# The pace of a second stream of work in a mixer: 1.2 of its steps for each step, where 0.89 were

## The chip, the cores and the metric

The kernel runs on one core of one Trainium2 chip. The metric is the time of one execution on the device in microseconds (us). Three executions of the kernel before took 3313.83, 3315.23 and 3316.35 us, so the median is 3315.23 us.

## What is computed

A transformer block (attention, a gated unit, a feed-forward net) works on `x`, 256 tokens of width 1024. Then two layers of a second network work on `x` and on a context `ctx` of 256 tokens. Each layer is a mixer and a layer of experts. Only the first of the two updates the context, and the mixer of the second layer needs the updated context for its keys and values. Cut to what matters:

```python
for i in range(2):
    update_ctx = i < 1
    x, ctx = mixer_sublayer(x, ctx, ...)      # attention, Fourier and convolution branches, three gates
    x = x + gt2 * peer_ffn(modulate(rmsnorm_2(x, g), sh2, sc2), ...)
    if update_ctx:
        ctx = ctx + cgt2 * peer_ffn(modulate(rmsnorm_2(ctx, g), csh2, csc2), ...)

def peer_ffn(h, ...):                          # per token 8 heads x 16 of 16384 experts
    eid, gate = top-16 of the product keys     # route
    u = jnp.take(u_tab, eid, axis=0)
    act = gelu(einsum('chkd,cd->chk', u, hc)) * gate
    v = jnp.take(v_tab, eid, axis=0)
    return einsum('chk,chkd->cd', act, v)
```

## The kernel before

All work is written as Python generators whose steps are recorded one after the other. There are two streams. The main stream takes `x` through the block and the two layers. The side stream takes the context through the first layer; it is advanced a step at a time between steps of the main stream (`alongside`, line 252). How many side steps a main step lets in is a number of the table `PACE` by phase: the first where the main step split a block of weights, the second where it did not (the steps of attention). A credit is added up, and a side step runs for each whole unit. The recorded instructions are then put in an order for each engine by a scheduler with a timeline of its own, so that instructions stand where that timeline had them, not strictly where they were recorded; each engine works through its queue in that order.

Phases that the text speaks of, with the stretch of the profiled execution that each fills:

- **First mixer** (`mix0`, 855 to 1166 us): `_mixer`, line 1012. Products with weights in blocks of 512 KB: each is loaded by the SP queue, split into a high part by ACT (line 364) and a low part by DVE (line 373), and multiplied in three passes on PE (lines 379 to 381, helper `mm3`). The branches (gates, Fourier, convolution) are woven with attention, whose eight heads go in two halves of four (`attend`, line 858: scores line 869, softmax lines 643 to 647, transposes line 540, outputs line 880). The outputs are merged and projected (lines 1082 and 535).
- **Routing** (`route0`, 1166 to 1354 us): a norm, a query product, scores (line 1124) and the top-16 search on DVE (lines 1091 to 1177). The scores of the first experts (tile `pre`, weights `uT`) are pulled forward by the scheduler and keep PE busy here.
- **Gates** (`gate0`, 1354 to 1506 us): for each of 32 groups of 8 tokens DVE builds one-hot tiles (lines 1373, 1374) and weighs them (line 1376, twice), PE multiplies them (line 1382), ACT evicts them (line 1384). The result goes to DRAM (`G`) and is read back in tiles `Gq`.
- **Dense experts** (`dense`, 1506 to 2165 us): products with `Gq` (line 1415), 128 blocks of `v` and the remaining score blocks on PE.
- **Second mixer** (`mix1`, 2165 to 2478 us): as the first. Its attention needs the keys of the updated context. So its attention is woven in only once the side stream has passed the word "keys" (`self.ready`, and `weave`, line 266, at half a step of attention for each step of the branches); whatever is left of attention when the branches end follows after them. The word comes after the very last piece of the context's experts.

The side stream in these phases, for two tiles of 128 tokens (`context_peer`): for each of 128 picks a row of `u` per token is fetched by an indirect DMA that POOL issues (line 1221, 512 KB each, tile `ug`, four buffers) and DVE reduces it (line 1234, `gather_acts`); then the rows of `v` are fetched and summed. For tile 0 the sum is made on PE (line 1289, tile `gacc`: a pair of fetches, then four matmuls, with line 1277 and 1304 on DVE around them). For tile 1 it is made on DVE (line 1254, one instruction for a fetch). The keys of tile 0 (`keys_tile`, line 934) come before the sum of tile 1, the keys of tile 1 at the end, and then the word "keys". A step of the side stream holds one fetch. A fetch also waits for the last split of weights that the main stream had recorded (`behind`, line 292), so that the pace holds on the chip too.

A mixer has 76 steps, 54 with a split of weights and 22 without (4 of keys, 4 of queries and 8 of heads, and 6 of the convolution).

Of the kernel before, what the change touches and what calls it, by code (L numbers as in the profile page):

```python
# [24 lines left out]
NCAND = 112  # L25
GSCALE = 2.0 ** 15
GATHER = (0,)
PACE = {"b1": (2.15, 2.48), "ffn": (1.8, 2.2), "mix0": (0.89, 0.89), "route0": (1.47, 1.25), "gate0":
        (1.16, 0.29), "pre0": (0.9, 1.4), "out0": (1.0, 2.8), "mix1": (0.7, 0.85)}
LOW = {"cmix": "V", "croute": "V", "keys": "V", "b1": "V", "b1r": "V", "ffn": "V", "mix0": "V", "route0":  # L30
       "V", "gate0": "V", "pre0": "V", "out0": "V", "mix1": "V", "route1": "P", "gate1": "V", "pre1": "VP",
# [166 lines left out]
class Net:  # L198
# [42 lines left out]
    def alongside(self, lead, side):  # L241

        credit = 0.0
        for step in lead:
            if step is not None:
                side.mark = step.ins
            credit += PACE[self.phase][step is None]
            while credit >= 1.0:
# [1397 lines left out]
```

## Time and profile before

| | |
|---|---|
| median of three executions | 3315.23 us |
| the profiled execution | 3327.51 us |
| its span in the profile | 3325.8 us |
| PE busy | 2955.7 us (89% of the span) |
| DVE busy | 2464.6 us (74%) |
| ACT busy | 1406.6 us (42%) |
| POOL busy | 806.3 us (24%) |
| granted TensorE clock, mean over the span | 0.937 |

The shares are means over stages with different limits. A row of a table by stage has the stretch, its length, and for each engine the time it was busy with the number of instructions in brackets, then the granted share of TensorE's full clock, the mean busy share of the 16 DMA engines and the rate that they moved. A row of waits has the instruction that waited, what it waited for, the total in us, how many times, and the longest. PE is the matmul unit, PEld its loading of weights, DVE the vector engine, ACT the scalar engine, POOL the engine that issues the indirect DMAs, SP the queue that loads weights.

### The profile page before, as it was taken

The numbers are of one execution on the slowest core, as the hardware profiler recorded it, in microseconds if no ns is written. First come the engines' busy times: TensorE is split into PE (matmuls) and PEld (weight loads), VectorE is DVE, ScalarE is ACT, GpSimd is POOL, SyncE is SP. The second block draws the span as 40 slices with busy tenths as digits, with TensorE's granted clock in tenths as the row PEclk, the third lists the DMA queues.
The fourth block names the chain that finished last, engine by engine and source line by source line (L and its number), as shares of the span: only waits on it lengthen the run. The fifth ranks groups of instructions, "written<-read, shape, count | busy, mean of one in ns | idle before, by whom it ended". The sixth has DMA issues, their size and how long they took to land.

```text
span 3325.8 us, 52744 instructions
## 1 busy us (share of the span) xinstructions
PE 2955.7 (89%) x19879; PEld 2532.1 (76%) x19879; DVE 2464.6 (74%) x5129; ACT 1406.6 (42%) x1938; POOL 806.3 (24%) x565
## 2 busy tenths in 40 slices
PE   6889997888799899947999899977889899999998
PEld 4777786778676677835888788866669899888998
DVE  2645659999896468997988788968657897655555
ACT  2444553333434343423445444443534454544443
POOL 0000000344443233433542444511004433000000
PEclk8999988899799889958999999989989999999999
DMA  7776633799987578988998899966444489755664
GB/s 245 252 251 236 214 133 121 274 329 327 361 297 253 187 268 309 341 293 329 378 368 296 324 370 365 356 223 223 140 137 137 146 250 297 264 193 192 211 215 153
DMA packets 289327, 852.87 MB, mean 256 GB/s; under 512 B 25264, under 2 KB 91568, under 8 KB 284592
## 3 DMA queue, kind: packets, MB, share of 16 engines
q1 hardware_dynamic: 147888, 543.16, 46.9%
q0 software_dynamic: 73728, 268.47, 21.9%
q10 hardware_dynamic: 67456, 37.88, 3.8%
q8 instruction: 156, 2.56, 0.3%
q14 instruction: 99, 0.81, 0.1%
HBM read 814.80 MB, written 34.60 MB: 255 GB/s over the span
## 4 chain that ended last, share of the span: by engine, by line
PE 55%; DVE 18%; DMA 14%; issue 8%; ACT 3%; POOL 2%; SPq 0%; ACTq 0%; DVEq 0%; POOLq 0%
PE acc L380 7%; PE acc L381 7%; PE acc L379 6%; PE ps L381 6%; PE ps L379 6%; PE ps L380 6%; DVE wl L373 4%; DMA ug<-in_u_dram,eidi 3%; DMA ug<-in_v_dram,eidT 3%; DMA w<-in_w_in_dram 3%; DVE gz L1234 2%; DMA w<-in_w_mod_dram 2%; PE pre L381 2%; DVE A L1376 2%; PE pre L379 2%
## 5 line engine op out<-in xcount | busy, mean ns | idle before, releaser
L364 ACT ACTIVATE wh<-w 128x1024 fp32r<-128x1024 f32 (+1 forms) x818 | 850.5, 1045 | 1039.4 <-PE ps L380 283.2
L373 DVE TENSOR_TENSOR wl<-w,wh 128x1024 fp32r<-128x1024 f32 (+1 forms) x770 | 928.4, 1207 | 447.8 <-PE ps L381 109.7
L379 PE MATMUL ps<-hh,wh 128*128 128x256 f32 x2304 | 663.9, 289 | 26.1 <-ACT wh L364 11.0
L381 PE MATMUL ps<-hh,wl 128*128 128x256 f32 x2304 | 666.8, 290 | 20.9 <-DVE wl L373 20.5
L380 PE MATMUL ps<-hl,wh 128*128 128x256 f32 x2304 | 659.9, 287 | 3.0 <-DVE hl L524 2.9
L1221 POOL DMA_INDIRECT ug<-in_u_dram,eidi x256 | 347.4, 1357 | 1007.2 <-DVE rstd L480 562.0
L379 PEld LDWEIGHTS ps<-hh,wh 128*128 128x128 f32 x2304 | 447.8, 194 | 54.5 <-issue 18.7
L381 PEld LDWEIGHTS ps<-hh,wl 128*128 128x128 f32 x2304 | 447.1, 194 | 45.0 <-DVE wl L373 31.2
L380 PEld LDWEIGHTS ps<-hl,wh 128*128 128x128 f32 x2304 | 447.7, 194 | 12.6 <-issue 4.9
L380 PE MATMUL acc<-wl,dh 128*128 128x512 f32 x1024 | 409.4, 400 | 23.6 <-DVE wl L373 23.5
L379 PE MATMUL acc<-wh,dh 128*128 128x512 f32 x1024 | 404.7, 395 | 14.3 <-ACT dh L523 12.2
L381 PE MATMUL acc<-wh,dl 128*128 128x512 f32 x1024 | 403.5, 394 | 0.5 <-DVE dl L524 0.5
L1234 DVE SCALAR_TENSOR_TENSOR gz<-ug,htok 128x1024 bf16<-128x1024 f32 x256 | 310.6, 1219 | 19.8 <-DMA ug<-in_u_dram,eidi 19.4
L381 PE MATMUL pre<-hh,wl 128*128 128x256 f32 x1024 | 299.5, 296 | 19.8 <-DVE wl L373 11.6
L379 PE MATMUL pre<-hh,wh 128*128 128x256 f32 x1024 | 292.5, 287 | 0.1
L380 PE MATMUL pre<-hl,wh 128*128 128x256 f32 x1024 | 292.4, 287 | 0.0
L1221 POOL DMA_INDIRECT ug<-in_v_dram,eidi x128 | 183.7, 1435 | 326.7 <-ACT wh L364 196.7
L380 PEld LDWEIGHTS acc<-wl,dh 128*128 128x128 f32 x1024 | 194.7, 190 | 76.6 <-DVE wl L373 40.6
L379 PEld LDWEIGHTS acc<-wh,dh 128*128 128x128 f32 x1024 | 194.8, 190 | 56.9 <-ACT dh L523 12.5
L381 PEld LDWEIGHTS pre<-hh,wl 128*128 128x128 f32 x1024 | 198.0, 195 | 40.9 <-DVE wl L373 17.7
L381 PEld LDWEIGHTS acc<-wh,dl 128*128 128x128 f32 x1024 | 194.7, 190 | 39.7 <-DVE dl L524 1.2
L373 POOL TENSOR_TENSOR wl<-w,wh 128x1024 fp32r<-128x1024 f32 x48 | 129.8, 2705 | 390.6 <-ACT wh L364 193.2
(514 smaller groups left out, 5112.2 us busy)
## 6 DMA issues: line engine op xcount, KB each, us to landing
w<-in_uT_dram SPq DMA_DIRECT2D x256, 512.0 KB, 4.7
w<-in_v_dram SPq DMA_DIRECT2D x256, 512.0 KB, 4.4
w<-in_w_in_dram SPq DMA_DIRECT2D x142, 512.0 KB, 4.7
w<-in_w_mod_dram SPq DMA_DIRECT2D x96, 512.0 KB, 5.0
w<-in_w_ff_dram SPq DMA_DIRECT2D x64, 512.0 KB, 5.8
G<-Gs ACTq DMA_DIRECT2D x32, 1024.0 KB, 7.9
Gq<-G SPq DMA_DIRECT2D x32, 1024.0 KB, 7.2
w<-in_w_ada_dram SPq DMA_DIRECT2D x48, 512.0 KB, 4.5
```

Of the source, the lines that this page charges most:

```text
L364: self.step = nc.scalar.activation(hi[:, :n], w[:, :n], AF.Copy)
L373: eng.tensor_tensor(lo[:, :n], w[:, :n], hi[:, :n].bitcast(F32), op=OP.subtract)
L379: mm(out, a[0], b[0], start=start, stop=False, skip_group_check=True)
L380: mm(out, a[0], b[1], start=False, stop=False, skip_group_check=True)
L381: mm(out, a[1], b[0], start=False, stop=stop, skip_group_check=True)
L1221: f = self.nc.gpsimd.indirect_dma_start(out=t, out_offset=None, in_=tab, in_offset=bass.IndirectOffsetOnAxis(ap=idx, axis=0))
L1234: nc.vector.scalar_tensor_tensor(j, ut, 1.0, ht, op0=OP.mult, op1=OP.mult, accum_out=sc[:, k:k + 1])
L1376: nc.vector.tensor_tensor(A2[:, i], ohA, over(gp[:, i, ts]), op=OP.mult)
```

## The change

One entry of the table of paces: in the first mixer 1.2 side steps are let in for a step of the main stream, of either kind.

```diff
-PACE = {"b1": (2.15, 2.48), "ffn": (1.8, 2.2), "mix0": (0.89, 0.89), "route0": (1.47, 1.25), "gate0":
+PACE = {"b1": (2.15, 2.48), "ffn": (1.8, 2.2), "mix0": (1.2, 1.2), "route0": (1.47, 1.25), "gate0":
         (1.16, 0.29), "pre0": (0.9, 1.4), "out0": (1.0, 2.8), "mix1": (0.7, 0.85)}
```

Nothing else is edited. 76 steps at 0.89 let in 67 side steps and at 1.2 let in 91, so from there on the side stream stands 24 steps further at every point, and 24 fewer are left at the end. Of 27 side steps that the second mixer took, it takes 3.

Three places show how the queues of the engines change. The first is PE's queue at the end of attention in the first mixer: `po` and `vc`, `v` are outputs of attention, `oh` and `ol` its split result in the projection that follows, and `gacc<-ug,gz` four matmuls for a pair of fetched rows. Before:

```order
L880 MATMUL po<-cpq,vc_92 64x256 x2
L880 MATMUL po<-cpq,v_9799 64x256 x2
L540 MATMUL ptx<-cst,prob 128x128 x8
L880 MATMUL po<-cpq,vc_92 64x256 x2
L880 MATMUL po<-cpq,v_9799 64x256 x2
L379 MATMUL ps<-oh,wh 128x256 x2
```

The same place in the changed program:

```order
L1289 MATMUL gacc<-ug,gz 32x512 x4
L880 MATMUL po<-cpq,vc_92 64x256 x2
L880 MATMUL po<-cpq,v_9833 64x256 x2
L540 MATMUL ptx<-cst,prob 128x128 x4
L1289 MATMUL gacc<-ug,gz 32x512 x4
L540 MATMUL ptx<-cst,prob 128x128 x4
L880 MATMUL po<-cpq,vc_92 64x256 x2
L880 MATMUL po<-cpq,v_9833 64x256 x2
L1289 MATMUL gacc<-ug,gz 32x512 x4
L379 MATMUL ps<-oh,wh 128x256 x2
```

Pairs of fetched rows now stand among the last heads. Counted over the whole queue, 27 pairs stood ahead of the last projection of the mixer and 32 do now; 31 stood ahead of the norm that begins routing and 39 do now; 35 stood ahead of the first routing score (line 1124) and 47 do now.

The second place is DVE's queue where routing ends and the first one-hot tile of the gates is built (line 1373): `oh` are the one-hots of routing, `iT` and `gp` its results, `wl` a split of weights for the scores, and `gz,sdot<-ug,htok` the reduction of one fetched row of `u`. Before:

```order
L1167 TENSOR_TENSOR oh<-iota16b,abr 128x256 x8
L373 TENSOR_TENSOR wl<-w,wh 128x1024
L1169 TENSOR_TENSOR oh<-oh,i16f 128x256 x8
L373 TENSOR_TENSOR wl<-w,wh 128x1024
L1171 TENSOR_REDUCE i_11408<-oh 128x128
L373 TENSOR_TENSOR wl<-w,wh 128x1024 x2
L1334 CAST iT<-ps 128x128 x2
L1335 TENSOR_SCALAR gT<-ps 128x128
L1336 CAST gp<-gT 128x128
L1337 TENSOR_TENSOR gp<-gT,gp 128x128
L1360 CAST iotaT<-cst 128x256
L1373 TENSOR_TENSOR ohB<-iotaT,iT 128x1024
```

The same place in the changed program:

```order
L1171 TENSOR_REDUCE i_11526<-oh 128x128
L1234 SCALAR_TENSOR_TENSOR gz,sdot<-ug,htok 128x1024 x2
L1334 CAST iT<-ps 128x128 x2
L1335 TENSOR_SCALAR gT<-ps 128x128
L1234 SCALAR_TENSOR_TENSOR gz,sdot<-ug,htok 128x1024 x2
L1336 CAST gp<-gT 128x128
L1234 SCALAR_TENSOR_TENSOR gz,sdot<-ug,htok 128x1024
L1337 TENSOR_TENSOR gp<-gT,gp 128x128
L1234 SCALAR_TENSOR_TENSOR gz,sdot<-ug,htok 128x1024
L1360 CAST iotaT<-cst 128x256
L1234 SCALAR_TENSOR_TENSOR gz,sdot<-ug,htok 128x1024
L1373 TENSOR_TENSOR ohB<-iotaT,iT 128x1024
```

Counted over the queue, no reduction of a row stood in routing and 40 stood between the first one-hot and the last weighing of the gates; now 35 stand in routing and 29 in the gates, 24 more in the two together. In the dense phase 88 of line 1234 and 105 of line 1254 become 64 and 127; in the second mixer 22 of line 1254 become none.

The third place is PE's queue in the second mixer, where the third head of the first half of attention ends: `htok` holds the context's values, `ps<-oh` is the projection after attention and `ps<-hh` a product of the branches. Before:

```order
L540 MATMUL ptx<-cst,prob 128x128 x4
L869 MATMUL sc<-cT,q_22581 128x256
L869 MATMUL sc<-k_22582,q_22581 128x256
L540 MATMUL ptx<-cst,prob 128x128 x4
L379 MATMUL ps<-oh,wh 128x256 x2
L815 MATMUL sc<-wa,cnT 128x512
L380 MATMUL ps<-ol,wh 128x256
L381 MATMUL ps<-oh,wl 128x256
L380 MATMUL ps<-ol,wh 128x256
L381 MATMUL ps<-oh,wl 128x256
L880 MATMUL po<-cpq,htok 64x256 x2
L880 MATMUL po<-cpq,v_22583 64x256 x2
```

The same head in the changed program:

```order
L381 MATMUL ps<-hh,wl 128x256
L379 MATMUL ps<-hh,wh 128x256
L380 MATMUL ps<-hl,wh 128x256
L381 MATMUL ps<-hh,wl 128x256
L379 MATMUL ps<-hh,wh 128x256
L380 MATMUL ps<-hl,wh 128x256
L880 MATMUL po<-cpq,htok 64x256 x2
L880 MATMUL po<-cpq,v_21870 64x256 x2
L540 MATMUL ptx<-cst,prob 128x128 x4
L815 MATMUL sc<-wa,cnT 128x512
L381 MATMUL ps<-hh,wl 128x256
L379 MATMUL ps<-hh,wh 128x256
```

The outputs of all four heads of the first half now stand among products of the branches, where before the branches had ended ahead of them. The second half of attention stands behind the branches in both.

## Rows read from the trace of the kernel before

**Rows 1.** Busy time by stage: the two mixers, routing, gates and dense experts between them.

```profile
855.00:1166.00 311.00, 268.31 (x1803) 205.61 (x1803) 218.31 (x551) 124.17 (x197) 113.24 (x96) 0.91 0.75 267
1166.00:1354.00 188.00, 174.42 (x1298) 141.10 (x1295) 150.52 (x586) 73.03 (x93) 70.47 (x63) 0.94 0.82 293
1354.00:1506.00 152.00, 101.49 (x899) 87.50 (x898) 144.83 (x232) 56.39 (x87) 53.61 (x43) 0.74 0.92 313
1506.00:2165.00 659.00, 617.46 (x3532) 531.47 (x3529) 565.23 (x685) 280.14 (x340) 293.55 (x196) 0.97 0.93 350
2165.00:2478.00 313.00, 259.88 (x1722) 214.43 (x1722) 218.89 (x575) 127.18 (x213) 27.19 (x21) 0.90 0.51 176
```

The columns behind the stretch and its length are PE, PEld, DVE, ACT, POOL, the granted clock, the DMA share and GB/s.

**Rows 2.** What PE waited for in routing and gates, 1166 to 1506 us.

```profile
PE gt L1382 <- DVE A L1376: 48.7, 38, 6.1
```

**Rows 3.** Chain of waits, end of the gates: start, us, what.

```profile
1503.14 1.67 PE gt L1382 x14
...
1529.67 0.50 PE acc L380
```

**Rows 4.** Waits in the second mixer's first half, 2165 to 2310 us.

```profile
POOL ug L1221 <- ACT wh L364: 98.7, 15, 28.9
ACT wh L364 <- DMA w<-in_w_in_dram: 26.4, 12, 6.5
DVE htok L1254 <- DMA ug<-in_v_dram,eidi: 19.7, 8, 6.1
...
ACT mt L517 <- DVE mt L514: 11.0, 2, 9.5
```

**Rows 5.** Busy time of line 1289 alone in the first mixer: PE, PEld.

```profile
855.00:1166.00 311.00, 37.04 (x248) 5.70 (x248) 0.91 0.75 267
```

**Rows 6.** What POOL waited for in the first mixer, the longest two.

```profile
POOL ug L1221 <- ACT wh L364: 50.4, 14, 22.0
POOL ug L1221 <- PE gacc L1289: 40.4, 11, 6.1
```

**Rows 7.** What PE waited for in the first mixer, the longest.

```profile
PE gacc L1289 <- DMA ug<-in_v_dram,eidT: 13.2, 8, 2.4
```

**Rows 8.** First mixer, busy time: last heads of attention, then the projections.

```profile
1074.00:1125.00 51.00, 40.37 (x210) 22.89 (x209) 23.13 (x82) 14.92 (x32) 10.32 (x11) 0.87 0.45 153
1125.00:1166.00 41.00, 37.20 (x297) 32.31 (x296) 23.67 (x31) 14.62 (x16) 13.51 (x10) 0.96 0.69 249
```

**Rows 9.** Busy time of line 1234 alone in the gates: DVE.

```profile
1354.00:1506.00 152.00, 48.71 (x80) 0.74 0.92 313
```

**Rows 10.** DVE at the end of a half sum of the context, in time order.

```profile
1178.49 1.62 DVE L1304 SCALAR_TENSOR_TENSOR cT<-gacc,mod_b_mod,cT 128x64 f32<-128x64 f32 x8
```

**Rows 11.** Busy time at the end of routing.

```profile
1300.00:1354.00 54.00, 50.76 (x408) 41.73 (x405) 45.59 (x117) 20.15 (x23) 24.44 (x20) 1.00 0.89 316
```

**Rows 12.** Dense experts: a stretch without and one with the context's keys.

```profile
1700.00:1800.00 100.00, 96.31 (x596) 84.70 (x595) 88.06 (x117) 44.54 (x54) 44.26 (x30) 1.00 0.98 366
1800.00:1900.00 100.00, 87.91 (x549) 77.45 (x550) 77.05 (x125) 46.04 (x64) 33.58 (x22) 0.98 0.79 286
```

**Rows 13.** Second mixer, busy time in five stretches.

```profile
2165.00:2192.00 27.00, 17.24 (x76) 14.11 (x77) 17.55 (x45) 10.27 (x19) 2.14 (x2) 0.56 0.39 137
2192.00:2258.00 66.00, 59.37 (x450) 53.11 (x449) 47.36 (x96) 26.12 (x41) 13.97 (x11) 0.95 0.75 267
2258.00:2384.00 126.00, 100.00 (x687) 84.28 (x685) 96.52 (x278) 54.64 (x85) 11.08 (x8) 0.92 0.55 187
2384.00:2443.00 59.00, 48.47 (x230) 31.52 (x229) 34.85 (x130) 23.25 (x55) 0.00 (x0) 0.91 0.13 45
2443.00:2478.00 35.00, 34.80 (x289) 31.42 (x287) 22.60 (x30) 12.90 (x15) 0.00 (x0) 1.00 0.65 211
```

**Rows 14.** Chain of waits, second mixer, end of attention's first half.

```profile
2398.73 1.96 PE po L880 x8
```

## The prediction

> **What bounds the kernel now.** I read the page, then busy time by stage, then the waits of each stage that the change reaches, then the chain of waits at its seams. From the table by stage the reader is to see that no engine is the bound throughout [rows 1]. In the dense phase PE is busy 617 of 659 us. In the gates DVE is busy 144.8 of 152 us and PE only 101.5, at a granted clock of 0.74 (1 would be 2.4 GHz throughout, 0.5 is 1.2). In routing and gates PE waited 48.7 us for the weighing on DVE [rows 2]. The dense phase cannot start before the gates have gone to DRAM and back: the last gate product is at 1503.1 us and the first product of the dense phase on the chain at 1529.7 [rows 3]. So a microsecond more of DVE ahead of that seam is a microsecond more of the whole. The mixers are bound by no one engine: the second has PE busy 259.9 of 313 us and DVE 218.9. It carries 23 fetches of the side stream whose reductions stand in DVE's queue and wait there for their rows, 19.7 us in all, with the mixer's own splits and norms behind them [rows 4].
>
> **The change, part by part.** The 24 side steps leave the second mixer and appear in the first; each phase between keeps its number of side steps but gets others of the list, 24 further on. Four terms follow.
>
> *First mixer and query: +13 us.* By PE's queue eight more pairs of fetches (39 for 31) stand ahead of the norm of routing, and four more between it and the first routing score, twelve in all. A pair costs PE 37.04/31 = 1.19 us (248 records are 31 pairs) [rows 5], so 14.3 us. POOL can issue them earlier: it waited 50.4 us for the pace and 40.4 us for PE to free a buffer [rows 6]. Five of the twelve stand among the last heads, where PE is idle 51.0 - 40.4 = 10.6 us [rows 8]; three of these I call hidden, -3.6 us. PE waited 13.2 us for rows over 31 pairs, 0.43 us each [rows 7]; half of that for twelve is +2.6. Both ends: 0 (all in the mixer's idle PE, 311.0 - 268.3 = 42.7 us) and 20 (nothing hidden, waits in full, 19.4). SP's loads share the DMA engines with the fetches. The projections move 249 GB/s x 41 us = 10.2 MB [rows 8]; about five pairs of 1.05 MB more make 15.4 MB, 377 GB/s. Stretches of the trace reach 366 [rows 12], so this is close to full but I add nothing.
>
> *Routing and gates: +22 us.* Ahead of the seam stand 24 more reductions of line 1234. One costs 48.71/40 = 1.22 us [rows 9], so 29.2 us. The eight instructions that end the context's half sum leave for the first mixer, -1.6 us [rows 10]. That makes 27.6 us. The cover is DVE's idle time from where the first of them stands, about 1300 us: 54.0 - 45.6 = 8.4 us [rows 11] and 152.0 - 144.8 = 7.2 us [rows 1], 15.6 us. It is made of short waits between dependent instructions, and the new ones wait for rows of their own, with the one-hots and the splits for PE behind them. I take a third of it as filled: 27.6 - 5.2 = 22. Both ends: 12 (all filled) and 28. PE's scores are ready early either way, so PE gains nothing here.
>
> *Dense experts: +8 us.* One reduction costs the same for tile 0 and 1, so 64 and 127 cost what 88 and 105 did. New is most of the context's second keys, which stood in the second mixer. The first keys are in this phase already, and the 100 us with them have PE busy 8.4 us less than the 100 before [rows 12]. I take one such loss. Both ends: 0 and 12.
>
> *Second mixer: -36 us.* By stretches [rows 13]:
> - Norm, 27 us. ACT waited 9.5 us at once for a DVE step [rows 4] that stood behind reductions. These go, but small steps of the keys stand there now: -5 (0 to -9.5).
> - First eighteen blocks of weights, 66 us for 450 products. ACT waits 26.4 us for weights in this half [rows 4], beside fetches that now are gone. At the rate of the last stretch, 289 in 35 us, they would need 54.5 us, 11.5 less. I take -8 (0 to -11.5).
> - Branches, 126 us with PE busy 100. The first half of attention, whose last heads end at 2400.7 us [rows 14], 16.7 us after the stretch, is now woven in: about +15 us for PE. The second keys leave, -8.4 as priced above, and of the 26 us in which PE stood idle half is filled by heads: -13. Sum -6 (+8 to -20).
> - End of attention, 59 us: those 16.7 us go, -17; the other half stays as it is.
> - Projections: PE busy 34.8 of 35 us, 0.
>
> The ends of this term are -9 and -53, the last being all the time that PE was idle (313 - 259.9).
>
> The sum is +13 + 22 + 8 - 36 = +7 us. It is made against the profiled execution (3327.5 us, span 3325.8); the median of the runs is 12.3 us less, 0.4%, which changes a difference of 7 us by nothing. 3315.2 + 7 = 3322 us.
>
> A rule is weighed here. In the mixer's second stretch PE reads as 90% busy and in the last as 99%, while products go at 6.8 and 8.3 in a microsecond [rows 13]: busy time hides a slower pace. The Trainium skill says so in "Perfetto Trace Analysis", section "Identifying the Most-Contended Engine": matmul busy time is a poor measure of the room left, and the busy share of the weight loads is a better one. The trace agrees: 31.4 of 35 us against 53.1 of 66. By that measure the mixer could shrink to 214.4/0.9 = 238 us, 75 us less and not 53, and the sum would be -32 at the utmost.
>
> **The rivals.**
> - *The second mixer fills up (faster).* Attention's first half disappears into the branches without lengthening them, as PE's rate in the last stretch allows. For it: that rate, and 26.4 us of waits for weights. Against it: the first mixer, woven that way already, takes 311 us, if with 31 pairs and 36 reductions in it. Price: the mixer gives -53 or a little over, the rest as above: -10; with the routing's gaps filled too, -20. Centre -16, 3299 us. It decides where the mixer falls under 265 us.
> - *The gather cannot keep up (slower).* The order is fixed but the rows come no faster: four buffers, and POOL already waits for PE to free them [rows 6]. Then DVE stands in routing at each reduction until its row lands, and the one-hots queue behind it. For it: fetches went at 63 in 188 us there [rows 1], 3.0 us each, and 24 would have to come sooner. Against it: few waits of PE for rows (13.2 us) [rows 7]. Price: 24 x 0.43 us of waits in routing, 20 for the first mixer in full, 28 for routing: 20 + 28 + 10 + 8 - 36 = +30, 3345 us. It decides once DVE waits over 10 us for rows ahead of the gates.
> - *Routing has room (no change).* The reductions fill all the gaps of 15.6 us; 13 + 12 + 8 - 36 = -3, 3312 us. The change then moves work and its time cancels. For it: DVE is idle 37.5 us of routing as a whole [rows 1]. Against it: they stand only in its last third.
>
> **How the numbers follow.** A measurement of this kernel tells about 0.2%, 6.6 us, from no change. My own case (0 to +17) has a chance of 0.44, of which 0.16 lies within 6.6 us and 0.28 above. The full mixer has 0.24, nearly all faster; the late gather 0.18, slower; routing with room 0.14, of which 0.12 is within and 0.02 faster. So faster 0.25, same 0.29, slower 0.46. My own case alone is 3315 to 3332. The range reaches to -25 and +33, that is 3290 to 3348, and leaves out some two in ten: the deep ends of the mixer's term and of the late gather.
>
> **What would show it.** Right: the second mixer shorter by 25 to 45 us with the first half of the heads (line 880) before the branches end and no line 1254; the seam of gates and dense phase later by 25 to 45 us after the start, with DVE busy throughout and some 24 more of line 1234 ahead of it; the first mixer longer by about 8 us. Wrong: a seam that hardly moves, a dense phase that grows by more than 12 us, or a second mixer still over 300 us.

## The result and the profile after

The changed kernel takes 3343.64 us (median of ten runs) against 3315.79 us of the kernel before (ten runs): ratio 1.0065, 95% interval 1.0047 to 1.0083, so 16 to 28 us slower. (The medians are 27.9 us apart; the means, 3342.9 and 3321.3 us, are 21.6 us apart, which is the ratio.) The profiled execution took 3345.57 us, 18.1 us more than that of the kernel before. The forecast was +7 us, in a range of -25 to +33.

The stages after, as in [rows 1]: the two mixers with routing, gates and dense experts between them. The columns are those of [rows 1].

```profile
858.00:1177.00 319.00, 275.47 (x1863) 206.89 (x1863) 221.93 (x566) 125.06 (x199) 122.47 (x113) 0.91 0.83 287
1177.00:1410.00 233.00, 193.78 (x1390) 161.95 (x1390) 192.97 (x654) 81.31 (x102) 108.57 (x87) 0.89 0.85 302
1410.00:1541.00 131.00, 90.65 (x737) 77.64 (x738) 127.13 (x200) 48.84 (x77) 35.41 (x27) 0.67 0.83 278
1541.00:2230.00 689.00, 633.07 (x3608) 544.48 (x3606) 581.66 (x714) 293.66 (x364) 285.98 (x192) 0.96 0.90 336
2230.00:2493.00 263.00, 243.52 (x1652) 202.53 (x1651) 177.34 (x498) 118.19 (x191) 0.00 (x0) 0.93 0.48 159
```

So that stages can be compared, each is cut at the same instruction in every kernel: a mixer runs from its memset (line 1026) to its last residual (line 535), the gates end with the last weighing (line 1376). By this cut the dense phase of the kernel before ends at 2171 us, not at the 2165 of [rows 1]. Lengths in us, with the runs of the experiments below (the dense phase begins where the second column ends):

| kernel | first mixer to end of gates | dense experts | second mixer | ratio to before |
|---|---|---|---|---|
| before | 650.5 | 665.6 | 306.5 | |
| after | 682.6 | 688.9 | 263.2 | 1.0065 |
| e1_keys_early | 682.9 | 712.5 | 256.4 | 1.0112 |
| e2_dense_takes | 649.7 | 747.0 | 257.0 | 1.0131 |
| e3_routing_spared | 648.2 | 658.4 | 306.8 | 1.0005 |
| e4_late_weave | 681.0 | 690.6 | 270.2 | 1.0085 |
| e5_less_before_more_after | 650.3 | 661.7 | 316.0 | 1.0020 |
| e6_no_second_keys | 684.5 | 665.3 | 256.4 | 0.9962 |
| e7_narrow_reductions | 657.9 | 681.3 | 262.7 | 0.9979 |
| e8_keys_back_in_mixer | 683.1 | 653.0 | 292.9 | 1.0023 |
| f1_quicker_end | 643.1 | 664.5 | 300.8 | 1.0018 |
| f2_dense_a_little_more | 651.7 | 666.8 | 289.3 | 0.9969 |
| f3_chain_among_blocks | 678.7 | 648.0 | 275.8 | 0.9983 |
| g1_keys_at_fourteen | 644.7 | 682.2 | 291.0 | 1.0011 |

One trace stands behind each row, and rows with the same side steps in a column spread. In the first column it is 643.1 to 651.7 us with the first mixer at 0.89 (before, e2, f1, f2, g1) and 678.7 to 684.5 with it at 1.2 (after, e1, e4, e6, e8, f3). In the second it is 658.4 to 665.6 (before, e3, f1) and 681.3 to 690.6 (after, e4, e7). There a difference under some 8 us between two rows is no effect by itself. In the third column such rows agree within 1 us (before and e3, after and e7).

From before to after: +32.1, +23.3, -43.3, and 6.0 us outside them (3.2 ahead of the first mixer, where nothing was moved and where the traces spread by 10 us; 2.8 behind the second). That is the 18 us. The two outer terms came about as forecast. The middle one did not: 23 us where the prediction had 8 with an end at 12.

**Ahead of the seam.** Line 1234 on DVE, in routing and in the gates after (DVE, granted clock, DMA share, GB/s), the answer to [rows 9]:

```profile
1177.00:1410.00 233.00, 41.99 (x69) 0.89 0.85 302
1410.00:1541.00 131.00, 35.90 (x60) 0.67 0.83 278
```

77.9 us for 48.7: 29.2 us more, as counted. The first routing score came at 1228.5 us for 1209.8. Waits of routing and gates after, beside [rows 2]:

```profile
PE gt L1382 <- DVE A L1376: 37.2, 38, 7.2
...
PE ps L540 <- DVE i L1171: 16.7, 2, 14.2
...
PE pre L381 <- DVE wl L373: 11.0, 10, 3.3
DVE gz L1234 <- DMA ug<-in_u_dram,eidi: 9.2, 13, 1.5
...
PE gacc L1289 <- DMA ug<-in_v_dram,eidT: 6.2, 8, 1.9
```

PE waits for DVE: less now for the weighing, more for splits, and 16.7 us for the result of the top-16 search (line 1171), which it did not wait for before. DVE waits 9.2 us in all for rows: they come nearly in time.

**The seam of dense phase and second mixer.** Up to the last additions to the dense activations (line 1415) the two kernels keep step: the last stands 647 us after the gates for 646. What is new comes behind it. The chain of waits after, from there to the second mixer:

```profile
2199.02 0.44 PE acc L380
2199.54 1.23 DVE wl L373
2200.76 1.05 DVE cT L1264 x4
2201.86 0.67 PE gacc L540 x4
2202.55 1.14 DVE cT L1264 x4
2203.82 3.56 PE gacc L945 x16
2209.53 0.30 DVE mt L950
2209.86 0.81 PE gacc L951 x2
2210.77 0.70 DVE mt L954
...
2212.66 2.02 ACT mt L958 x5
2214.68 0.53 ACT kh L523
2215.25 0.58 PE gacc L379
...
2219.97 0.21 PE gacc L380
2220.78 0.23 PE acc L380
```

The dense product `acc` stops at 2199.5 us and, one product apart, goes on at 2220.8. For these 21 us PE's queue holds the context's last sum (line 1264), its norm (945 to 954) and its key products, small steps that wait for each other from engine to engine; the last of the dense products, and the residual of `x` with them, stand behind. The rows themselves are not late: the last of their sums (line 1254) ends at 2196.7 us, and in the 20 us ahead of it DVE has no wait for a row. The end of the dense phase (the columns of [rows 1] again), after, and below it in e6_no_second_keys, which lacks the chain: PE is busy 28.9 of 43 us at a granted clock of 0.76, and without the chain 37.5 of 40 at 1.00.

```profile
2187.00:2230.00 43.00, 28.89 (x134) 23.33 (x132) 26.48 (x68) 19.56 (x34) 0.05 (x1) 0.76 0.38 131
```

```profile
2164.00:2204.00 40.00, 37.51 (x224) 30.80 (x222) 37.44 (x61) 17.61 (x24) 11.04 (x8) 1.00 0.90 314
```

**The second mixer.** The same chain stood there before. The stretch from the 192nd to the 216th product of line 379 with `hh`, first before, then after:

```profile
2294.00:2339.00 45.00, 28.80 (x176) 23.80 (x177) 38.25 (x143) 16.56 (x27) 3.63 (x3) 0.77 0.41 146
```

```profile
2339.00:2358.00 19.00, 19.00 (x138) 16.24 (x137) 15.19 (x47) 10.88 (x17) 0.00 (x0) 1.00 0.60 201
```

26 of the 43 us that the mixer gave back are this stretch; before, it also held four sums of rows and 12 instructions of the mixer's convolution (line 918), 11 us of DVE. The dense phase took 23 of the 43.

### The profile page after: what moved, and what is told of

Same layout as the page of the kernel before. It is cut to its first block, busy times and chain, and to the rows that moved or that the text cites. A ratio compares the mean times of both kernels' runs of the same rounds, so it can differ in the third digit from the quotient of the medians.

```text
span 3343.9 us, 52730 instructions
## 1 busy us (share of the span) xinstructions
PE 2974.0 (89%) x19879; PEld 2547.5 (76%) x19879; DVE 2468.1 (74%) x5129; ACT 1412.4 (42%) x1940; POOL 804.3 (24%) x565
## 4 chain that ended last, share of the span: by engine, by line
PE 57%; DVE 19%; DMA 14%; issue 5%; ACT 3%; POOL 1%; SPq 0%; DVEq 0%; ACTq 0%; POOLq 0%
PE ps L381 7%; PE acc L380 7%; PE ps L379 7%; PE ps L380 7%; PE acc L381 6%; PE acc L379 6%; DVE wl L373 4%; DMA ug<-in_u_dram,eidi 4%; DMA ug<-in_v_dram,eidT 3%; DMA w<-in_w_in_dram 2%; DVE gz L1234 2%; DVE A L1376 2%; DVE ohB L1373 2%; DMA w<-in_w_mod_dram 2%; PE pre L381 1%
## 5 line engine op out<-in xcount | busy, mean ns | idle before, releaser
L1221 POOL DMA_INDIRECT ug<-in_u_dram,eidi x256 | 336.3, 1314 | 1037.9 <-DVE rstd L480 564.0
L379 PE MATMUL pre<-hh,wh 128*128 128x256 f32 x1024 | 295.8, 291 | 4.8 <-ACT more L1400 3.1
L1221 POOL DMA_INDIRECT ug<-in_v_dram,eidi x128 | 192.8, 1506 | 240.9 <-ACT wh L364 117.0
L379 PEld LDWEIGHTS acc<-wh,dh 128*128 128x128 f32 x1024 | 194.1, 190 | 57.2 <-ACT dh L523 12.6
```

The source lines that it names most:

```text
L379: mm(out, a[0], b[0], start=start, stop=False, skip_group_check=True)
L1221: f = self.nc.gpsimd.indirect_dma_start(out=t, out_offset=None, in_=tab, in_offset=bass.IndirectOffsetOnAxis(ap=idx, axis=0))
```

## The experiments

Each run is timed against runs of the kernel before on the same chip. "1.2" is the changed kernel; a diff shows what differs from it, where nothing else is said.

**e1_keys_early**

```diff
-"out0": (1.0, 2.8)
+"out0": (1.08, 2.8)
```

> The pace of the first mixer stays 1.2; the pace of the dense phase goes from 1.0 to 1.08, so that the word 'keys' comes 13 of 208 steps (some 40 us) before the dense phase ends and not in the third step of the second mixer. Theory (the seam of dense and second mixer): in the changed kernel the context's last keys, a chain of dependent small steps, stand in the queues ahead of the last products and the residual of the dense phase, and the stretch from the last weighing of the gates to the second mixer is 689 us for 666 for that reason alone. Moved inside they have cover, so some 15 of those 23 us come back: 3328 us, ratio to the kernel before 1.002 to 1.006, the stretch about 674 us. Rival (the dense phase is full: each side step in it costs wherever it stands): nothing comes back, 3344 us or a little more, ratio 1.0065 or above.

Measured: 3358.5 us, ratio 1.0112 (1.0087 to 1.0136), dense phase 712.5 us. It went the wrong way: the ratio is in the rival's range, but for another reason. What PE waited for from 2140 to 2200 us, the longest two:

```profile
PE gacc L540 <- DVE htok L1254: 14.2, 1, 14.2
PE gacc L379 <- ACT kh L523: 4.6, 1, 4.6
```

and the busy time from 2170 on:

```profile
2170.00:2190.00 20.00, 6.57 (x26) 5.42 (x26) 9.77 (x25) 1.26 (x2) 1.63 (x2) 0.50 0.19 57
```

The last sum of a row (line 1254) ends 635 us after the gates, 21 us sooner than in the changed kernel (656), but the transposes that begin the chain stand earlier still in PE's queue. So PE stands 14 us for it and then runs the chain at the lower clock, 1.2 GHz. This place inside the dense phase was no cover.

**e2_dense_takes**

```diff
-"mix0": (1.2, 1.2) ... "out0": (1.0, 2.8)
+"mix0": (0.89, 0.89) ... "out0": (1.2, 2.8)
```

> The first mixer back at 0.89; the dense phase at 1.2 for 1.0, so that it takes the 24 steps (and the last four) in place of first mixer, routing and gates, and the word 'keys' comes 13 steps before its end. Theory (the loss of the change is DVE work ahead of the seam of gates and dense phase, the gain is the second mixer): the gates end at 1506 us as in the kernel before, the second mixer falls from 306 to some 263 us, and the dense phase pays by its DMA: 24 fetches of 0.52 MB at its 353 GB/s are 36 us at most, if its 0.94 DMA share is full, and 8 us for the keys if not: 3316 - 43 + 8 to 36 = 3281 to 3309, I take 3297, ratio 0.990 to 0.998. Rival (the side work costs about the same wherever it stands, so that only its place in the sum changes): 3343, ratio 1.006 or above.

Measured: ratio 1.0131 (1.0102 to 1.0161). The seam of the gates stands as before (649.7 us) and the mixer falls to 257, as the theory said; the dense phase pays 81 us and not 8 to 36; the ratio is in the rival's range. The two longest waits of PE that are new:

```profile
PE gacc L540 <- DVE htok L1254: 29.9, 1, 29.9
...
PE gacc L945 <- ACT gz L943: 12.2, 1, 12.2
```

The first is at the chain: PE stands while DVE makes the last 16 sums of rows. The second is at the first keys. In all PE is idle 107 us of this dense phase, for 45 before, and busy 20 us longer; what the rest of the 81 us is was not followed.

**e3_routing_spared**

```diff
-"route0": (1.47, 1.25)
+"route0": (0.8, 0.65)
```

> The first mixer at 1.2; routing at 0.8 and 0.65 for 1.47 and 1.25, which lets in 27 side steps and not 51, so that gates, dense phase and second mixer stand where they did in the kernel before. Theory: only the first mixer's own term is left, +8 us by the trace of the changed kernel (319 for 311), and routing has eight pairs of fetches less and no reductions, so it is up to 10 us shorter than the 188 us of before: 3316 + 8 - 10 to 0 = 3314 to 3324, ratio 0.9995 to 1.0025. Rival (the gather cannot keep up in the first mixer, and what is late there is what lengthens routing): routing stays some 20 us or more above 188 although it has fewer steps, 3335 us or above, ratio over 1.005.

Measured: ratio 1.0005 (0.9988 to 1.0023), and first mixer to end of gates 648.2 us for 650.5. By the cut of [rows 1] routing is 224 us long, as in the rival, but the gates are 111: the first one-hot stands later, the seam does not. The first mixer at 1.2 costs nothing at the seam if routing lets in as many steps less. In this run what counts is how many side steps stand ahead of the seam, not where.

**e4_late_weave**

```diff
-WEAVE = (..., (0, 0.5), (0, 2.0))
+WEAVE = (..., (26, 0.5), (0, 2.0))
```

> As the changed kernel, but attention of the second mixer is woven in only from the 26th step of its branches on, where the kernel before had it. Theory (prediction): of the 43 us that the second mixer gave back, the fetches' leaving gave 13 (norm 5, first blocks 8) and attention's earlier place the other 30: 3344 + 30 = 3374 us, the mixer about 293 us, ratio to the kernel before 1.013 to 1.018. Rival (the fetches and their reductions leaving gave nearly all of it): 3344 to 3354 us, the mixer at most 275 us, ratio under 1.0115.

Measured: ratio 1.0085 (1.0057 to 1.0113), second mixer 270.2 us for 263.2. The rival was right: attention's earlier place is worth 7 us in the trace, and the timed runs can hardly tell it from nothing. The edit takes back most of the earlier place, not all: the outputs of the first four heads (line 880) stand behind 261, 301, 306 and 306 products of line 379, where it was 304, 304, 306 and 306 before and is 239, 251, 269 and 282 in the changed kernel.

**e5_less_before_more_after**

```diff
-"mix0": (1.2, 1.2) ... "mix1": (0.7, 0.85)
+"mix0": (0.75, 0.75) ... "mix1": (0.95, 1.15)
```

> The other way round: the first mixer at 0.75 for 0.89, so that it lets in 57 side steps and not 67, and the second mixer at 0.95 and 1.15 for 0.7 and 0.85, so that it takes 37 and not 27 and 'keys' still comes at its 37th step. Theory (prices per step from the runs so far: 24 steps ahead of the seam of gates and dense phase cost 35 us, 1.47 each; in the second mixer 24 steps cost 43 - 26 = 17 us beside the keys, 0.7 each): 10 x (1.47 - 0.7) = 8 us faster, 0.9975 of the kernel before, 0.996 to 0.999. Rival (in the second mixer the gather is what is late, and more steps in the same stretch wait longer): no gain or a loss, 1.000 to 1.005, the second mixer at 320 us or more for 306.

Measured: ratio 1.0020 (1.0005 to 1.0036). This is in the rival's range. Ten steps fewer ahead of the seam gave nothing (650.3 us for 650.5): the first mixer is 11 us shorter, and what follows up to the end of the gates 11 us longer. So 1.47 us a step is no price that holds on both sides of 0.89. In routing PE waited 19.9 us for fetched rows there:

```profile
PE gacc L1289 <- DMA ug<-in_v_dram,eidT: 19.9, 7, 5.8
```

The row of the same view before has 10.2 us. That this is what ate the gain was not tried.

**e6_no_second_keys**

```diff
+        if l == 1 and tt == 1:
+            for a in range(4):
+                nc.vector.tensor_copy(vc()[:, tt, 2 * a:2 * a + 2, :].rearrange("p h d -> p (h d)"), x[:, a, ts])
+            for _ in range(4):
+                yield None
+            return
         gs = self.gs(scale, "g_norm1" + s, f"k{tt}")
```

> As the changed kernel, but the chain that makes the second keys of the context is left out: four copies of the context's sum into the values stand in its place (so the keys and values of 128 context tokens are not the reference's), and they wait for the same last fetches. Theory (the 23 us by which the dense phase is longer are the key chain, standing in the queues ahead of the last products): the dense phase falls from 689 to 666 to 670 us, the ratio to the kernel before from 1.0065 to 1.000, 0.998 to 1.002. Rival (the dense phase is longer because the last fetches are late, whatever stands behind them): it stays at 683 us or above, ratio 1.0045 or above.

Measured: ratio 0.9962 (0.9946 to 0.9977), dense phase 665.3 us for 688.9 and 665.6. The 23 us are the key chain: the last fetches are the same ones here, and the transposes of their sum (line 540) still stand in PE's queue, where PE waits 0.35 us. The second mixer is 7 us shorter as well; the end of the chain (lines 976 to 994), which reaches into it in the changed kernel, is left out too.

**e7_narrow_reductions**

```diff
+            w = 128 if tt == 1 and k < 32 else 1024
-            nc.vector.scalar_tensor_tensor(j, ut, 1.0, ht, op0=OP.mult, op1=OP.mult,
+            nc.vector.scalar_tensor_tensor(j[:, 0:w], ut[:, 0:w], 1.0, ht[:, 0:w], op0=OP.mult, op1=OP.mult,
```

> As the changed kernel, but the first 32 reductions of the second tile, which stand in routing and gates, work on 128 of 1024 columns (so those 32 picks get part of their product); the fetches and all else are the same. They take some 31 us from DVE ahead of the seam, about what 24 more reductions added. Theory (DVE's work ahead of the seam sets it): the seam, at 1541 us in the changed kernel, comes back to 1506 to 1518, ratio to the kernel before 0.996 to 1.001. Rival (the rate of the fetches, DMA or POOL, sets it): the seam stays at 1533 or later, ratio 1.0045 or above.

Measured: ratio 0.9979 (0.9961 to 0.9998). The reductions (now line 1235) in routing and gates:

```profile
1178.00:1374.00 196.00, 5.86 (x40) 0.97 0.88 315
1374.00:1522.00 148.00, 42.61 (x88) 0.68 0.91 302
```

48.5 us for 77.9: 29.4 less on DVE, and first mixer to end of gates 657.9 us for 682.6, 24.7 less. The seam is at 1522 us only because this trace begins the first mixer at 864. The narrowed reductions begin behind the first routing score. From there to the end of the gates it is 294.3 us, where the changed kernel has 312.4 and the kernel before 295.8: these 18 us are DVE's work, as the fetches are the same. The other 6.6 us lie ahead of the first score, where nothing was edited (363.6 us from the mixer's start, 366.5 to 370.2 in the six others at 1.2); what they are was not followed.

**e8_keys_back_in_mixer**

```diff
-"out0": (1.0, 2.8)
+"out0": (0.9, 2.8)
```

> As the changed kernel, but the dense phase at 0.9 for 1.0: it lets in 187 side steps and not 208, and the second mixer 24 and not 3, with the word 'keys' at its step 33. Theory (the keys cost some 25 us wherever they stand behind the last fetch; a fetch costs the dense phase little, since PE bounds it): the dense phase is 660 to 668 us, the second mixer 300 to 308, and with 35 us ahead of the seam the ratio is 1.009 to 1.012. Rival (a fetch costs the dense phase as much as it does routing and gates, 1.47 us): the dense phase is 635 to 645 us, ratio 1.002 to 1.006.

Measured: ratio 1.0023 (1.0009 to 1.0038), dense phase 653.0, second mixer 292.9 us. The ratio is in the rival's range, the stages fit neither price: 21 steps fewer than before are 12.6 us in the dense phase, 0.6 us each, by two single traces. Three steps fewer in the second mixer, with "keys" at its step 33 and not 37, are 14 us.

**f1_quicker_end**

```diff
-"mix0": (1.2, 1.2) ... "mix1": (0.7, 0.85)
+"mix0": (0.89, 0.89) ... "mix1": (0.95, 1.15)
```

> The kernel before (first mixer at 0.89) with the second mixer at 0.95 and 1.15 for 0.7 and 0.85: its 27 side steps are let in sooner and 'keys' comes at its step 28, still among its blocks of weights, and not at 37. Theory (the key chain costs some 25 us where the main stream has nothing else ready, and less among blocks of weights, which PE has work for; attention is woven in earlier besides, 7 us by the run with the late weave): the second mixer takes 285 to 295 us for 306, ratio to the kernel before 0.994 to 0.997. Rival (the last fetches cannot come sooner, and PE waits for them at the chain): the mixer stays at 304 us or above, ratio 0.9995 or above.

Measured: ratio 1.0018 (1.0000 to 1.0036), second mixer 300.8 us. Not faster; in the trace six of the hoped-for 11 to 21 us came.

**f2_dense_a_little_more** (f1 with one number more)

```diff
-"out0": (1.0, 2.8)
+"out0": (1.04, 2.8)
```

> As the run before it, and the dense phase at 1.04 for 1.0, which takes 8 more side steps, so that the second mixer takes 19 and has 'keys' at step 19. Theory (a side step costs the dense phase 0.6 us as long as the gather keeps up, as the run with 21 fewer showed): dense phase 666 + 5 = 671 us, second mixer 275 to 288, ratio 0.992 to 0.997. Rival (at a pace over 1.0 the gather falls behind in the dense phase, as at 1.2, and each step more costs 2 us or over): dense phase 680 us or longer, ratio 0.998 or above.

Measured: 3311.04 us, ratio 0.9969 (0.9954 to 0.9985), dense phase 666.8, second mixer 289.3 us. This one beats both kernels, by some 10 us the one before.

**f3_chain_among_blocks**

```diff
-"out0": (1.0, 2.8), "mix1": (0.7, 0.85)
+"out0": (0.96, 2.8), "mix1": (0.95, 1.15)
```

> As the changed kernel (first mixer at 1.2), with the dense phase at 0.96 and the second mixer at 0.95 and 1.15: the last 12 side steps stand in the second mixer and the word 'keys' at its step 12, among the eighteen blocks of weights at its start. Theory (the chain is covered there): the seam of gates and dense phase stays at +35 us, the dense phase is 656 to 664 us, the second mixer 265 to 280 us for 263 with nothing in it: ratio to the kernel before 0.998 to 1.003, some 15 us less than the changed kernel. Rival (the chain costs its 23 us there too): the second mixer 286 us or longer, ratio 1.005 or above.

Measured: ratio 0.9983 (0.9967 to 1.0000), dense phase 648.0, second mixer 275.8 us. The ratio and the mixer are the theory's. The mixer is 12.6 us longer than in the changed kernel, six sums of rows (7.6 us of DVE) included, and 19.4 us longer than in e6, which has no second keys at all; on the seam the whole chain cost 30 us by e6 (23.6 in the dense phase, 6.8 in the mixer). So among the blocks a part of it is covered. The stretch with the chain, from the 72nd to the 96th product of line 379 with `hh`, and under it the same stretch in the changed kernel, which has no chain there:

```profile
2237.00:2271.00 34.00, 19.18 (x109) 16.75 (x110) 34.00 (x122) 10.05 (x24) 0.00 (x0) 0.70 0.25 78
```

```profile
2271.00:2282.00 11.00, 10.24 (x84) 9.04 (x83) 9.24 (x24) 7.17 (x18) 0.00 (x0) 1.00 0.71 241
```

The 23 us between them are not the chain's price. DVE is busy all the while, mostly with the main stream's convolution (line 918, busy DVE alone, in the same two stretches):

```profile
2237.00:2271.00 34.00, 23.61 (x52) 0.70 0.25 78
```

```profile
2271.00:2282.00 11.00, 4.32 (x10) 1.00 0.71 241
```

19 us of that work is done here that the changed kernel does later, and PE's longest wait, 10.5 us, is for a norm of the main stream (line 784). In f2 the stretch with the chain takes 43 us for 18, and holds 43 of these instructions for 22. With 199 steps the dense phase took 648 us and with the 187 of e8 653, so the 0.6 us per step of e8 is no price either.

**g1_keys_at_fourteen**

```diff
-"mix0": (1.2, 1.2) ... "out0": (1.0, 2.8), "mix1": (0.7, 0.85)
+"mix0": (0.89, 0.89) ... "out0": (1.065, 2.8), "mix1": (0.95, 1.15)
```

> The first mixer at 0.89, the dense phase at 1.065 for 1.0, the second mixer at 0.95 and 1.15: the dense phase takes 13 side steps more than in the kernel before, the second mixer 14, with the word 'keys' at its step 14. Theory (what the change gains is an earlier end of the context in the second mixer, what it loses stands ahead of the seam of gates and dense phase; both can be had by taking the steps into the dense phase as far as the gather keeps up, 0.6 us each): seam as in the kernel before, dense phase 667 to 676 us, second mixer 276 to 284 us for 306: ratio 0.991 to 0.996. Rival (at this pace the gather falls behind in the dense phase, and PE waits at the key chain, as it did for 14 us at 1.08 in the run with the keys early): dense phase and second mixer together no less than the 956 us that they took at 1.04, ratio 0.9965 or above.

Measured: ratio 1.0011 (0.9995 to 1.0026), dense phase 682.2 and second mixer 291.0 us. Five steps more than in f2 lose what f2 had won. The sum is the rival's, but its mechanism is not in the trace: PE has no long wait for a fetched row. 12 of the 16 us lie in the stretch with the first keys (122 us for 110). What it is stays open.

## Why the prediction held, and where it did not

The measured +16 to +28 us lies in the range of -25 to +33, but at or beyond the end of my own case (0 to +17). The range reached so far for the late gather (+30), which did not happen; that the time fell there for another reason is luck.

- *First mixer and query, +13 (0 to 20).* The first routing score stands 18.7 us later, 15.5 of them within the term. Right in size. The mixer itself is 7.7 us longer, as said.
- *Routing and gates, +22 (12 to 28).* From the first score to the end of the gates 312.4 us for 295.8: +16.6. The 24 reductions were counted right (29.2 us) and their cover was filled twice as far as I took, 11 us and not 5.2. Both terms together, 35 forecast, 32.1 measured; e7 shows that DVE is the cause (18 us of it, as narrow reductions gave them back), e3 that a first mixer at 1.2 need not move the seam.
- *Dense experts, +8 (0 to 12).* This is the step that failed: 23.3 us, and a growth of more than 12 us was named ahead as a sign of being wrong. I priced the second keys by the first ones, the 8.4 us of idle PE in [rows 12], and "I take one such loss". But the first keys, at 1799 us, follow a sum that PE had finished at 1372, while the second follow the last sum of a row 3 us behind it, and by the new pace they end exactly where the main stream has its own seam: nothing of `x` can start until the products behind the chain are done. e6 takes the chain out, and 23.6 us go with it. The sums of rows were not late there, so it is the chain's own length that the term lacked.
- *Second mixer, -36 (-9 to -53).* 43.3 measured by the cut used here. By parts: the first products of line 379 come 4 us sooner after the mixer's start (5 forecast), the eighteen blocks behind them gain 5 (8 forecast), the stretch with the keys 26 (8.4 of PE forecast there), and 8 are left for all the rest, where I had 17 for the end of attention alone; e4 gives 7 for attention's earlier place. The term was nearly right as a sum of two errors: the stretch with the keys was worth three times as much, the weaving, as far as e4 takes it back, less than half.
- *The rule on weight loads.* The Trainium skill, "Perfetto Trace Analysis", section "Identifying the Most-Contended Engine", takes the share of weight loads, with the rate of matmul work, as the measure of the room left; by it the prediction estimated that the mixer could fall to 238 us. It fell to 263, and to 256 in e1 and e6; in the changed kernel the loads are busy 202.5 us, 0.77 of it. That is short of the 0.9 of the estimate; what held it was not tried.
- *The rivals.* The first was to decide where the mixer, 313 us by the cut of [rows 1], falls under 265, by 48 us; it fell by 43.3, and the dense phase took half of it back. The late gather did not happen at this pace: DVE waited 9.2 us for rows in routing and gates, just under the 10 us from which it was to decide. e7 shows what the seam waited for: DVE's work. At 1.08 and 1.2 in the dense phase the last sums did come late for PE's queue (14.2 and 29.9 us in e1, e2). Routing had little room: the new work filled 11 of the 15.6 us, and the seam moved by 32 us.

So the size (+7 forecast) hangs on one term above all: with the 23 us that the dense phase lost in place of the 8, and all else as forecast, the sum would have been +22.

## What to carry to other kernels

Price the end of a side stream apart from its body: a chain of small dependent steps behind the last transfer costs its full length, here 23 us of the dense phase, where the queues hold it ahead of the last work before a seam of the main stream. Placed ahead of its data it cost more (e1, e2), among blocks of weights less (f3). A pace moves every later phase, so count at each seam how much more work of the engine that binds there now stands ahead of it. And find out how far the neighbouring phase can take steps (here 1.04, not 1.065) before you move them into a phase that is bound already; e1 and e2 lost more there than they saved.

## What was not expected of the hardware

Where PE stands still for such a chain, the granted clock falls with it: 0.50 over the 20 us of e1 (1.2 GHz throughout) and 0.53 over 47 us of e2, where PE was busy 7.4 us:

```profile
2149.00:2196.00 47.00, 7.43 (x28) 5.97 (x29) 26.21 (x39) 5.39 (x12) 16.14 (x13) 0.53 0.49 165
```

In e1 the key products that end the wait run at that level. In time order (start, us, instruction), two of them, and two products of the main stream with as many columns, 11 us later:

```profile
2198.91 0.41 PE L379 MATMUL gacc<-wh,kh 128*128 128x256 f32 x1
2199.13 0.41 PE L380 MATMUL gacc<-wl,kh 128*128 128x256 f32 x1
...
2210.13 0.28 PE L380 MATMUL ps<-hl,wh 128*128 128x256 f32 x1
2210.25 0.28 PE L381 MATMUL ps<-hh,wl 128*128 128x256 f32 x1
```

They follow each other at 0.22 us and at 0.12 us. So part of the chain's price is this clock: for its 24 key products an estimate of 24 x 0.10 = 2.4 us, from these rows.
